# A two-layer hybrid attention trunk: later rotation copies, a value tile between two scores, and four places in the queues

## The chip, the core and the metric

The kernel runs on one core of one Trainium2 chip. The core has a matrix engine (TensorE, "PE" in the profile; its weight loads are listed apart as "PEld"), VectorE ("DVE"), ScalarE ("ACT"), GpSimd ("POOL") and SyncE ("SP"). Each works through its own queue of instructions in the order in which they were put there, and a wait at the head of a queue holds up all behind it. In this kernel SP issues all the DMA transfers; "SPq" is its queue. The metric is the time of one execution of the whole program on the device, in microseconds (us); the median of the runs is given.

## The reference: what is computed

The trunk has two layers over one sequence of 1024 tokens of width 1024, in float32. In each layer a modulated RMSNorm gives `h`, a combined input projection feeds an attention, its output is gated with SiLU, and an output projection with a gate is added to `x`.

```python
for i in range(2):
    shift, scale, gate = modulation(c, ada_w[i], ada_b[i])      # silu(c) @ ada_w + ada_b
    h = rmsnorm(x, norm_g[i]) * (1 + scale) + shift
    y = diff_attention(h, ...) if i == 0 else mla(h, ...)
    x = x + gate * y
return rmsnorm(x, final_norm_g)

def diff_attention(h):                  # 8 heads, two 64-wide query/key pairs, values 128 wide
    q, k, v, z = split(h @ w_in0)
    q, k = rope(q), rope(k)             # x1*cos - x2*sin, x2*cos + x1*sin
    p = softmax(q k^T / 8)
    o = (p[0] - lam * p[1]) @ v
    return (rmsnorm(o) * silu(z)) @ w_out0

def mla(h):                             # 8 heads, 128 + 64 wide
    q_a, c_kv, k_pe, z = split(h @ w_in1)
    q = rmsnorm(q_a) @ w_q_b; k, v = split(rmsnorm(c_kv) @ w_kv_b)
    o = softmax((q_nope k_nope^T + rope(q_pe) rope(k_pe)^T) / sqrt(192)) @ v
    return (o * silu(z)) @ w_out1
```

## The kernel before

**Precision.** Every operand of a product is split into a high part (`fp32r`, made by a cast on ACT) and a low part (the difference, made by a subtraction on POOL or DVE), and a product of two tiles is three matmuls (`mm3`, lines 182 to 184): high by high, high by low, low by high.

**Start (to about 145 us).** `h0`, the transposed modulated input, is made in two halves of 512 tokens. Value tiles (`v0_tile`, line 737: 8 steps of `mm3` each, one tile for each 128 tokens and half of the value columns) are projected, cast by `store_v` (L362, L363) and stored to DRAM. The keys, queries and the gate z of head 0 are projected here. The loop `for tt in range(8)` (line 859) runs the value tiles of the second column half; between them it issues what `pend` holds, the rest of the rotation of head 0, and ahead of tile 6 (`V_LATE`) the score tile `q_tile(0, 0, 0, ...)` of head 0, which takes its banks from a new PSUM pool.

**First attention (to about 692 us).** `attn0` takes the heads in turn. A head has 8 query tiles. `q_tile` (line 837) issues for each of the two query/key pairs four score matmuls (L847), a row maximum on DVE (L400) and an exponential on ACT (L402), then the combination on DVE (L855). Then the tile before it is transposed on PE (L383), copied out by ACT (L385, `pth`) and DVE (L386, `ptl`), and multiplied by the values (`pv`). Between these parts PE gets fill work: `FILL0` says how many steps of `stream0` go where. `stream0` is the projection of the next head's keys, queries and z from `h0`: three strips for each head, two halves of 512 tokens for each strip, 8 steps (one `mm3` each) for each half, 48 steps for each head.

**The rotation.** When a half of keys or queries is complete, `rope` (line 312) copies it out of PSUM on ACT (`rp_raw`, L319 or L321), issues four transfers that exchange the 32-row blocks (`rp_sw`, L323), and multiplies by the cosines (L324). It returns two functions. `rot` multiplies the exchanged rows by the sines (L329) and, where `add` is POOL, adds the two on POOL (L331). `fin` adds them on DVE (L336) where `add` is DVE, and returns the sum `r`. Heads 1 to 7 of the first layer rotate with POOL alone, head 0 with DVE. `stack_k` (line 341) and `stack_q` (line 349) then make the operands of the scores: two casts of 64 rows on ACT (L344, L345; L352, L353), two subtractions on POOL (L346, L347; L354, L355), and for queries four transfers that copy the rows to the other half of the partitions (L357, L358).

**The side list.** `Side` (line 279) is a list from which one entry is taken at each step of `stream0` and once after each query tile; an entry is a function or nothing. `k_done` and `q_done` (lines 752 and 764) put 8 entries on it for each half: three empty, `rot`, three empty, and `g`, which calls `fin` and stacks.

**Order.** The program's order is not kept as it stands on every engine: the instructions are put in order for each engine at compile time by estimated times. `tc.issue_after(ins)` holds the instructions of a block behind `ins` where they are on the same engine; `tc.keep_in_program_order` (`in_turn`) fixes an instruction's place; `behind("S")` and `behind("V")` hold a cast or an addition behind the last softmax or transposed copy that was traced on that engine (`mk`).

**First output projection (about 660 to 790 us).** It is done with seven products of half-size blocks in place of eight (`Seven`). Each product needs operands that are split into high and low (`split_a`, `split_w`: a cast on ACT, L1171, a subtraction on POOL or DVE, L1172). In head 7, where `stream0` has run out, `extra0(i)` runs after query tile `i`: it fetches and splits the first product's operands and, by `PRE0`, issues steps of the first products (`pre0.step()`, one step at tile 4, two at tile 5 and so on).

**Second layer.** `group0` (line 1399) makes the second layer's `h1` for 512 tokens from eight chunks (`h_chunk`, line 459: four transposes on PE, a modulated cast on ACT, L473, the same value on DVE, L477, and a subtraction, L478); those of the first group go through the side list beside the last output products. `lora` (line 1621) projects the latent strips; it loads and splits a strip's weights with `strip1` (L206, then L227 on ACT and L228 on POOL) and needs the first two strips (`w4`, split earlier) before the third. Then `z_pair` (line 1756) makes the gates of three pairs of heads, again with seven products, and `load_wk` (line 1787) loads and splits the value weights, `fh` being the half of the columns: a cast on DVE (L1792), a subtraction on POOL (L1793). Raw weights share two buffers with the tag `wraw`. The second attention (about 976 to 1330 us) and the second output projection follow.

Of the kernel before, what the change touches and what calls it, by code (L numbers as in the profile page):

```python
# [16 lines left out]
ALU = mybir.AluOpType  # L17
# [20 lines left out]
DEF = 7  # L38
ROT = 3
# [5 lines left out]
V_LATE = 6  # L45
# [31 lines left out]
def f32v(ap):  # L77
    return ap.bitcast(F32)
# [3 lines left out]
def trunk(ctx: ExitStack, tc: tile.TileContext, A, out):  # L82
    nc = tc.nc
    SP, PE, V, S, G = nc.sync, nc.tensor, nc.vector, nc.scalar, nc.gpsimd
# [256 lines left out]
    def stack_k(t, r):  # L341

        with behind("S"):
            S.copy(t[0:64, 0, :], r[0:64])  # L344
            S.copy(t[64:128, 1, :], r[64:128])  # L345
        in_turn(G.tensor_sub(t[64:128, 0, :], r[0:64], f32v(t[0:64, 0, :])))  # L346
        in_turn(G.tensor_sub(t[0:64, 1, :], r[64:128], f32v(t[64:128, 1, :])))  # L347

    def stack_q(qa, qb, r):

        with behind("S"):
            S.copy(qa[0:64, 0, :], r[0:64])  # L352
            S.copy(qa[64:128, 1, :], r[64:128])  # L353
        in_turn(G.tensor_sub(qb[0:64, 0, :], r[0:64], f32v(qa[0:64, 0, :])))  # L354
        in_turn(G.tensor_sub(qb[64:128, 1, :], r[64:128], f32v(qa[64:128, 1, :])))  # L355
        for t in (qa, qb):
            SP.dma_start(f32v(t[64:128, 0, :]), f32v(t[0:64, 0, :]))  # L357
            SP.dma_start(f32v(t[0:64, 1, :]), f32v(t[64:128, 1, :]))  # L358
# [393 lines left out]
    def k_done(h):  # L752
        def f(acc, half):
            rot, fin = rope(wp, acc, half, 1.0, *[G if h else V] * 2)

            def g():
                t = a0a.tile([P, 2, HF], F32R, name="ks", tag="ks", bufs=4)
                stack_k(t, fin())
                KS.setdefault(h, [None, None])[half] = t

            side.add(*[None] * ROT, rot, *[None] * (DEF - 1 - ROT), g)
        return f

    def q_done(h):
        def f(acc, half):
            rot, fin = rope(wp, acc, half, SC0, *[G if h else V] * 2)

            def g():
                qa = a0a.tile([P, 2, HF], F32R, name="qa", tag="qs", bufs=4)
                qb = a0a.tile([P, 2, HF], F32R, name="qb", tag="qs", bufs=4)  # L770
                stack_q(qa, qb, fin())
                QS.setdefault(h, [None, None])[half] = qa, qb

            side.add(*[None] * ROT, rot, *[None] * (DEF - 1 - ROT), g)
        return f

    def silu_gate(tp, acc):

        th = tp.tile([P, HF], F32, name="zth", tag="rp", bufs=6)
        gz = wst.tile([P, HF], F32, name="gz", tag="gz", bufs=3)  # L780
        S.activation(th, acc, AF.Tanh, scale=0.5)
        V.scalar_tensor_tensor(out=gz, in0=th, scalar=1.0, in1=acc, op0=ALU.add, op1=ALU.mult)
        return gz

    def z_done(h):
# [73 lines left out]
    for tt in range(8):  # L859
        if tt == V_LATE:  # L860
            psum("ps2", sc=2, tr=1, pv=1)
            zz0 = sm.tile([P, 4], F32, name="zz")
            first += [zz0, q_tile(0, 0, 0, zz0, a0a)]
        for _ in range(MODS[tt]):
            next(mods_g)
        for t in pend[2 + 2 * tt : 4 + 2 * tt] if tt else ():
            t()
        v0_tile(tt, 1, wv1)
    assert next(mods_g, 0) == 0
    stm.close()  # L870

# [394 lines left out]
    def extra0(i):  # L1266
        nonlocal xp, pw
        if i < 4:
            gate_step0()
        if i == 1:  # L1270
            sv0.fetch_w(0, 0)
        if i < Z_LAST:
            return
        sv = sv0

        def fa(n, *hs):
            for h in hs:
                sv.fetch_a(n, h)

        def fw(n, *hs):  # L1280
            for h in hs:
                sv.fetch_w(n, h)

        def both(n, h):
            sv.split_a(n, h, G)
            sv.split_w(n, h)

        if i == Z_LAST:
            stream0.step(99)
            side.flush()  # L1290
            stW.close()
            stH.close()
            xp = pool(stX, "xp", side="right")
            pw = pool(stO, "pw0", side="right")
            k0["o"] = pw.tile([P, HF], F32, name="o7")
            k0["sq"] = wst.tile([P, HF], F32, name="sq7", tag="gz", bufs=3)
            for n in ("11", "21", "12"):
                k0[n] = pw.tile([P, HF], F32, name="k" + n)
            sv.kept[0][3], sv.kept[1][3] = k0["11"], k0["12"]
            fa(0, 0, 1)  # L1300
            fw(0, 1)
            sv.split_w(0, 0)
        if i == 3:
            sv.split_a(0, 0, G)
            fw(0, 2)
            fa(0, 2)
            fw(0, 3)
            tc.keep_in_program_order(SP.dma_start(k0["11"], oF[0][3, 0]))
        for n, h in ((), (), (), (), ((0, 1), (0, 2)), ((0, 3),), ((1, 0), (1, 1)), ((1, 2),), (), (), ())[i]:
            both(n, h)  # L1310
        while rests:
            rests.pop(0)()
        if i == 4:
            for h in range(2):
                fw(1, h)
                fa(1, h)
        if i == 5:
            fw(1, 2)
            fa(1, 2)
            fw(1, 3)  # L1320
        if i == 6:
            tc.keep_in_program_order(SP.dma_start(k0["21"], oF[0][3, 1]))
            k0["pair"] = [pw.tile([P, HF], F32, name="ob", tag="ob", bufs=4) for _ in range(4)]
            for t, (hh, half) in zip(k0["pair"], ((2, 0), (6, 0), (2, 1), (6, 1))):
                tc.keep_in_program_order(SP.dma_start(t, oF[0][hh, half]))
        if i == 8:
            sv.split_w(1, 3)
            a11, a12, a21, a22 = k0["pair"]
            for n, t in ((2, a11), (3, a22), (4, a12), (5, a21)):
                sv.kept[n][2] = t  # L1330
            k0["sum"] = combine(*k0["pair"])
        if i > 7:
            next(k0["sum"], None)
        for _ in range(PRE0[i]):
            pre0.step()
# [44 lines left out]
    def strip1(i, wpool=None):  # L1380
        return load_strip([A["w_s1"][i, f] for f in range(2)], [4, 4], wpool)
# [17 lines left out]
    def group0(gi):  # L1399
        fulls = [[x_] for x_ in xf[4 * gi : 4 * gi + 4]]  # L1400
        V.tensor_add(ssa[gi], ssa[gi], ssb[gi])
        norm_x(ssa[gi], fulls, (2, 3) if gi else (1, 3))

        def chunk(k):
            if gi == 1:
                h1[k][1] = xt2k("h1h"), xt2k("h1l")
                h1f[k] = ut(f"h1f{k}", dt=F32)
            else:
                h1[k][0] = [h1p.tile([P, HF], F32R, name="h1_" + x_, tag="h1", bufs=16) for x_ in "hl"]
            lm["V"] = h_chunk(1, fulls, k, h1[k][gi], p3x, V, f32=h1f[k] if gi else None)  # L1410

        if gi == 0:
            side.add(*[None] * G_WAIT)
        side.add(*[lambda k=k: chunk(k) for k in ((0, 4, 1, 5, 2, 6, 3, 7) if gi else range(KT))])
# [206 lines left out]
    def lora(idx, dst, gvec, width, ws=None, first=None):  # L1621
# [45 lines left out]
            norms.append(lambda: norms.append(rest))  # L1667

        for i, si in enumerate(idx):
            w = strip1(si) if i or ws is None else ws  # L1670
            for half in range(2):
                if (i, half) == (0, 0) and first:
                    first(lambda acc: put(0, 0, acc))
                else:
                    half_and_norm(w, half, lambda acc: put(i, half, acc))
                if i == n - 1:
                    norms.append(lambda half=half: norm(half))
# [109 lines left out]
    def load_wk(fh):  # L1787
        for k in range(2):
            raw = wst.tile([P, HF], F32, name="wvr", tag="wraw", bufs=2)
            SP.dma_start(raw, A["w_v1"][k, fh])  # L1790
            h_, l_ = [pv1.tile([P, HF], F32R, name="wv" + x_, tag="wv1", bufs=4) if fh else ut("wv" + x_, True) for x_ in "hl"]
            V.tensor_copy(h_, raw)  # L1792
            G.tensor_sub(l_, raw, f32v(h_))  # L1793
            wk[k][fh] = (h_, l_)

    def v1_tile(tt, fh, sp, *buf):
# [17 lines left out]
    def late_z(i):  # L1814
        if i == 0:
            load_ck(CK, 3, [(k, half) for half in range(2) for k in range(2)])
            for name, nk in (("w_qr", 3), ("w_kn", 2), ("w_qn", 3)):
                raw = p4.tile([P, HF], F32, name="zraw", tag="zraw", bufs=6)
                SP.dma_start(raw[:, : nk * P], A[name][0])
                kraw.append((raw, nk))  # L1820
        if i == 2:
            load_wk(0)
            load_ck(CQ, 0, [(i, half) for half in range(2) for i in range(3)])
            load_wk(1)

    z_pair(1)
    z_pair(2)
    z_pair(3, late_z)
    ws1 = [split_strip([raw]) for raw in kraw]
# [536 lines left out]
```

## Time and profile before

| | |
|---|---|
| time, median of 3 runs | 1434.04 us (1433.14 to 1435.34) |
| the profiled execution's own time | 1429.06 us |
| its span, first to last instruction | 1426.9 us |
| mean granted clock of TensorE | 0.992 |
| ACT, share of the span | 737.9 us, 52% |
| POOL, share of the span | 753.9 us, 53% |
| DMA, share of 16 engines' span | 51.0% |

Busy times come from the hardware profiler. Matmuls are pipelined, and their ends are modelled, so a busy PE can hide short gaps: a 128x512 matmul is listed with some 0.39 us, while the next one starts 0.22 us after it. In a row of the timeline the columns are the start and the length in us, the engine, the line, the operation, the tile written and the tiles read, shapes and count; in brackets how long the engine had stood idle and who ended that. In a row of the waits they are who waited (engine, tile, line) and for whom, then us in total, the number of waits and the longest. A row of the windows has the stretch, its length, the busy us of the five engines with their counts of instructions, the granted clock (1.00 is full), the share of the DMA engines and GB/s.

### The profile page before, as it was taken

The page shows a single profiled execution, that of the slowest core. Times are in us where ns is not written, and L with a number is a line of the kernel's source. Part 1 is how long each engine was busy: PE and PEld are TensorE (multiplying, and loading weights), DVE is VectorE, ACT ScalarE, POOL GpSimd, SP SyncE. Part 2 cuts the span into 40 slices and gives each one's busy share as a digit, 9 for nine tenths or more (in the row PEclk, how much of TensorE's full clock was granted, in tenths as well). Part 3 has the DMA queues.
Part 4 walks back from the last instruction along what each step waited for, and adds up shares of the span by engine and source line. Part 5 has one row for each costly group of instructions (what it writes and reads, how often), then busy time and mean ns, then how long its engine had stood idle before and what let it go on. Part 6 is the DMA issues. An engine that isn't in the chain of part 4 may idle for free.

```text
span 1426.9 us, 20750 instructions
## 1 busy us (share of the span) xinstructions
PE 1380.7 (97%) x7350; PEld 1150.1 (81%) x7350; DVE 937.0 (66%) x1337; ACT 737.9 (52%) x1331; POOL 753.9 (53%) x592
## 2 busy tenths in 40 slices
PE   8999999999999999999998999999999999999997
PEld 6767787888878788787786888887888888888886
DVE  7665668776766666667596886545666655555685
ACT  5523455655555556566555544335454454545554
POOL 5415263758685858576695232543131165653783
PEclk8999999999999999999999999999999999999999
DMA  9776634343434344425574126398544355566463
GB/s 341 250 237 191 203 91 116 103 143 90 155 116 131 122 135 132 139 70 173 174 252 155 45 75 229 109 305 251 159 124 121 102 162 189 181 212 205 141 246 119
DMA packets 149066, 231.54 MB, mean 162 GB/s; under 512 B 20577, under 2 KB 57569, under 8 KB 148962
## 3 DMA queue, kind: packets, MB, share of 16 engines
q1 hardware_dynamic: 148962, 230.21, 51.0%
q8 instruction: 58, 0.95, 0.3%
q14 instruction: 46, 0.38, 0.1%
HBM read 144.74 MB, written 61.81 MB: 145 GB/s over the span
## 4 chain that ended last, share of the span: by engine, by line
PE 70%; DVE 5%; POOL 5%; ACT 3%; DMA 3%; issue 2%; SPq 2%; POOLq 0%; ACTq 0%; DVEq 0%
PE s L1986 10%; PE acc L182 8%; PE acc L184 8%; PE acc L183 8%; PE tr L383 7%; PE s L847 6%; PE pv L182 3%; PE pv L184 3%; PE pv L183 3%; PE zacc L184 1%; PE zacc L183 1%; PE zacc L182 1%; PE oy L184 1%; PE oy L182 1%; PE oy L183 1%
## 5 line engine op out<-in xcount | busy, mean ns | idle before, releaser
L385 ACT CAST pth<-tr 128x512 fp32r<-128x512 f32 x256 | 150.1, 586 | 283.8 <-PE tr L383 280.6
L400 DVE TENSOR_REDUCE nm<-s 128x1 f32<-128x1024 f32 x192 | 233.9, 1219 | 77.4 <-PE s L847 68.1
L386 DVE TENSOR_TENSOR ptl<-tr,pth 128x512 fp32r<-128x512 f32 x256 | 176.1, 688 | 148.5 <-ACT pth L385 147.9
L228 POOL TENSOR_TENSOR wl<-wraw,wh 128x512 fp32r<-128x512 f32 (+2 forms) x79 | 102.1, 1295 | 185.0 <-ACT wh L227 180.8
L383 PE MATMUL tr<-ident,e 128*128 128x128 f32 x1024 | 155.8, 274 | 10.0 <-DVE ptl L386 9.7
L383 PEld LDWEIGHTS tr<-ident,e 128*128 128x128 f32 x1024 | 120.4, 140 | 54.3 <-DVE ptl L386 31.5
L402 ACT ACTIVATE e<-s,nm 128x1024 f32<-128x1024 f32 x128 | 143.6, 1121 | 26.5 <-DVE nm L400 26.2
L182 PE MATMUL acc<-h0h,wh 128*128 128x512 f32 x360 | 150.6, 418 | 0.1
L182 PE MATMUL pv<-pth,vt 128*128 128x256 f32 x512 | 147.5, 288 | 0.0
L183 PE MATMUL pv<-ptl,vt 128*128 128x256 f32 x512 | 145.5, 284 | 0.0
L184 PE MATMUL pv<-pth,vt 128*128 128x256 f32 x512 | 144.6, 282 | 0.0
L184 PE MATMUL acc<-h0h,wl 128*128 128x512 f32 x360 | 143.2, 398 | 0.4 <-POOL wl L228 0.4
L183 PE MATMUL acc<-h0l,wh 128*128 128x512 f32 x360 | 142.1, 395 | 0.0
L183 PEld LDWEIGHTS pv<-ptl,vt 128*128 128x128 f32 x512 | 97.6, 191 | 2.9
L182 PEld LDWEIGHTS pv<-pth,vt 128*128 128x128 f32 x512 | 97.4, 190 | 3.1 <-ACT pth L385 0.2
L184 PEld LDWEIGHTS pv<-pth,vt 128*128 128x128 f32 x512 | 97.6, 191 | 0.0
L329 POOL TENSOR_TENSOR rp_sw<-rp_sw,sinT 128x512 f32<-128x512 f32 x42 | 57.3, 1365 | 73.8 <-DMA rp_sw<-rp_raw 72.8
L324 POOL TENSOR_TENSOR rp_r<-rp_raw,cosT 128x512 f32<-128x512 f32 x38 | 49.8, 1312 | 86.4 <-ACT rp_raw L321 38.7
L1172 POOL TENSOR_TENSOR wol<-wol,woh 128x512 fp32r<-128x512 f32 x56 | 82.8, 1500 | 21.5 <-ACT woh L1171 18.8
L847 PE MATMUL s<-ks,qa 128*128 128x512 f32 x256 | 83.5, 407 | 5.9 <-DVE e L855 4.1
L855 DVE SCALAR_TENSOR_TENSOR e<-s,z,e 128x1024 f32<-128x1024 f32 x64 | 82.2, 1284 | 2.2
L847 PE MATMUL s<-ks,qb 128*128 128x512 f32 x256 | 80.7, 396 | 0.3 <-DMA qb<-qb 0.3
(411 smaller groups left out, 3484.3 us busy)
## 6 DMA issues: line engine op xcount, KB each, us to landing
ada<-in_ada_ss SPq DMA_DIRECT2D x32, 512.0 KB, 5.6
wraw<-in_w_s SPq DMA_DIRECT2D x64, 256.0 KB, 2.9
vS<-v_hl SPq DMA_DIRECT2D x32, 512.0 KB, 6.0
vt<-vS SPq DMA_DIRECT2D x32, 512.0 KB, 4.7
wol<-tS SPq DMA_DIRECT2D x56, 256.0 KB, 5.1
tS<-ob SPq DMA_DIRECT2D x48, 256.0 KB, 2.0
rp_sw<-rp_raw SPq DMA_DIRECT2D x168, 64.0 KB, 2.0
bc_s<-bc_d SPq DMA_DIRECT2D x34, 256.0 KB, 3.9
```

Of the source, the lines that this page charges most:

```text
L182: PE.matmul(psum, ah, bh, start=first, stop=False, skip_group_check=skip)
L183: PE.matmul(psum, ah, bl, start=False, stop=False, skip_group_check=skip)
L184: mm3.last = PE.matmul(psum, al, bh, start=False, stop=last, skip_group_check=skip).ins
L228: sub = (V if pair_of else G).tensor_sub(l_[:, :n], raw[:, :n], f32v(h_[:, :n]))
L383: transpose_p.last = PE.transpose(tr[:, j, :], p[:, kt * P : (kt + 1) * P], ident).ins
L385: mk["S"] = S.copy(pth[kh][:, :, dst], tr).ins
L386: mk["V"] = V.tensor_sub(ptl[kh][:, :, dst], tr, f32v(pth[kh][:, :, dst])).ins
L400: mk["V"] = V.reduce_max(nm, s_ps, axis=AX.X, negate=True).ins
L402: mk["S"] = S.activation(e, s_ps, AF.Exp, bias=nm, scale=1.0, accum_out=zs).ins
L847: PE.matmul(s_ps[:, kc * HF : (kc + 1) * HF], src[:, c, ql], KS[h][kc][:, c, :], start=fst, stop=not fst)
L1172: sub = eng.tensor_sub(lo, raw, f32v(hi))
L1986: PE.matmul(s_ps[:, kc * HF : (kc + 1) * HF], lhs, rhs(kc), start=i == 0, stop=i == 4)
```

## The change

For heads 1 to 7, `k_done` and `q_done` put two more entries on the side list ahead of `g`: one that calls `fin`, and an empty one, which the queries of heads 5 to 7 do without. In the start stage a value tile is put between the two scores of the first query tile, and `pend`'s functions are held behind the last gate product. In head 7 three splits change places. In `lora` the casts of all strips that it loads itself are held behind the ACT cast of the first group's last chunk. The value weights `fh = 1` are loaded one stage earlier, and their subtraction is on DVE.

```diff
@@ k_done
-                stack_k(t, fin())
+                stack_k(t, r.pop() if r else fin())
-            side.add(*[None] * ROT, rot, *[None] * (DEF - 1 - ROT), g)
+            r = []
+            sum_ = [lambda: r.append(fin()), None] if h else []
+            side.add(*[None] * ROT, rot, *[None] * (DEF - 1 - ROT), *sum_, g)
@@ q_done
-                stack_q(qa, qb, fin())
+                stack_q(qa, qb, r.pop() if r else fin())
-            side.add(*[None] * ROT, rot, *[None] * (DEF - 1 - ROT), g)
+            r = []
+            sum_ = [lambda: r.append(fin()), None][: 1 + (h < 5)] if h else []
+            side.add(*[None] * ROT, rot, *[None] * (DEF - 1 - ROT), *sum_, g)
@@ silu_gate
-        V.scalar_tensor_tensor(out=gz, in0=th, scalar=1.0, in1=acc, op0=ALU.add, op1=ALU.mult)
+        silu_gate.last = V.scalar_tensor_tensor(out=gz, in0=th, scalar=1.0, in1=acc, op0=ALU.add, op1=ALU.mult).ins
@@ for tt in range(8)
-            first += [zz0, q_tile(0, 0, 0, zz0, a0a)]
+            first += [zz0, q_tile(0, 0, 0, zz0, a0a, lambda c: None if c else v0_tile(V_LATE, 1, wv1))]
...
-            t()
-        v0_tile(tt, 1, wv1)
+            with tc.issue_after(silu_gate.last):
+                t()
+        if tt != V_LATE:
+            v0_tile(tt, 1, wv1)
@@ extra0
         if i == 3:
-            sv.split_a(0, 0, G)
...
-        for n, h in ((), (), (), (), ((0, 1), (0, 2)), ((0, 3),), ((1, 0), (1, 1)), ((1, 2),), (), (), ())[i]:
+        if i == 4:
+            sv.split_a(0, 0, G)
+            both(0, 1)
+            sv.split_a(0, 2, G)
+        if i == 5:
+            sv.split_w(0, 2)
+        for n, h in ((), (), (), (), (), ((0, 3),), ((1, 0), (1, 1)), ((1, 2),), (), (), ())[i]:
             both(n, h)
@@ group0, chunk
+            if gi == 0:
+                lm["h"] = h_chunk.act
@@ lora
-            w = strip1(si) if i or ws is None else ws
+            w = ws
+            if i or ws is None:
+                raws = fetch_strip([A["w_s1"][si, f] for f in range(2)], [4, 4])
+                with tc.issue_after(lm["h"]):
+                    w = split_strip(raws)
@@ load_wk
-            G.tensor_sub(l_, raw, f32v(h_))
+            (V if fh else G).tensor_sub(l_, raw, f32v(h_))
@@ late_z
             load_ck(CQ, 0, [(i, half) for half in range(2) for i in range(3)])
-            load_wk(1)
...
     z_pair(1)
+    load_wk(1)
     z_pair(2)
```

`both(n, h)` is `split_a(n, h, G)` and `split_w(n, h)`.

## The prediction

> **What bounds the kernel now.** I read the page first, then the list of waits, then windows by stage, and last the timeline around the stalls that the change touches.
>
> ```profile
> span 1426.9 us, 20750 instructions
> ...
> PE 1380.7 (97%) x7350; PEld 1150.1 (81%) x7350; DVE 937.0 (66%) x1337; ACT 737.9 (52%) x1331; POOL 753.9 (53%) x592
> ```
>
> TensorE (PE) is the bound from end to end: 1380.7 of 1426.9 us. No matmul is added or removed, so the change can only win from the 46 us in which PE stands, and from matmuls run at a lowered clock. The waits of PE and the two of ScalarE (ACT) that matter most (who waited for whom: us in total, times, longest):
>
> ```profile
> PE tr L383 <- DVE ptl L386: 9.7, 11, 2.2
> PE trh L468 <- DVE h L477: 4.5, 1, 4.5
> PE s L847 <- DVE e L855: 4.1, 7, 1.0
> PE ssq L924 <- ACT rp_raw L321: 2.5, 1, 2.5
> PE vps L182 <- DVE gz L782: 1.3, 1, 1.3
> PE s L847 <- DVE v_hl L363: 1.3, 1, 1.3
> PE acc L182 <- ACT rp_raw L321: 1.2, 1, 1.2
> ...
> PE vps L182 <- DVE v_hl L363: 0.7, 1, 0.7
> ...
> ACT qa L352 <- POOL rp_r L331: 23.3, 11, 4.8
> ACT ks L344 <- POOL rp_r L331: 8.2, 5, 3.4
> ```
>
> The pattern: ACT's queue is served in order, and the casts that stack a rotated half (qa, ks) stand at its head while GpSimd (POOL) still makes the rotation's sum, 31.5 us in all. Behind them stand the exponentials and the copies of transposed tiles (pth), on which DVE's ptl and e depend, and on these PE. The windows (length, then PE, PEld, DVE, ACT and POOL busy, granted clock, DMA share, GB/s) say where PE pays:
>
> ```profile
> 206.00:224.00 18.00, 14.24 (x80) 11.35 (x79) 12.83 (x17) 7.93 (x14) 9.14 (x8) 1.00 0.49 121
> ...
> 412.00:420.00 8.00, 5.50 (x26) 4.39 (x25) 4.62 (x9) 4.90 (x8) 7.77 (x7) 0.87 0.47 149
> ...
> 478.00:512.00 34.00, 30.74 (x159) 23.82 (x158) 23.68 (x33) 20.05 (x37) 26.37 (x22) 1.00 0.47 140
> ...
> 562.00:582.00 20.00, 17.57 (x94) 14.10 (x93) 12.85 (x18) 10.74 (x19) 14.31 (x13) 1.00 0.38 108
> ...
> 655.00:712.00 57.00, 51.45 (x303) 42.33 (x302) 37.62 (x59) 35.70 (x64) 36.47 (x31) 1.00 0.55 178
> ...
> 776.00:780.00 4.00, 2.96 (x10) 2.52 (x11) 3.79 (x6) 2.20 (x5) 0.20 (x1) 0.57 0.57 193
> ...
> 945.00:960.00 15.00, 15.00 (x68) 12.43 (x67) 8.34 (x13) 6.21 (x11) 3.60 (x3) 1.00 1.07 352
> ```
>
> Idle PE in the first four (length less PE busy): 3.76, 2.50, 3.26 and 2.43, together 11.95 us, all within the first attention. At 412 to 420 the clock was 0.87 as well, 8 x 0.13 = 1.0 us of matmul time lost.
>
> **1. The copies two steps later (heads 1 to 7).** For these heads the sum is already issued by `rot`, so the new list entry only returns the tile: no instruction is added, the stacking casts, their two POOL subtractions and, for queries, four SP transfers move back by two ticks of the side list (one for queries from head 5 on). A tick comes with each of 48 stream steps and 8 tiles of a head; the first qb score of head 6 stands at 569.62 and of head 7 at 640.31 (rows below), 70.7 us for 56 ticks, 1.26 us each. Each half's list grows from 8 entries to 10, against 9.3 ticks per half, so the list backs up by a step or two within a head and `rot` moves a little too.
>
> ```profile
> 211.90 0.62 ACT L352 CAST qa<-rp_r 64x512 fp32r<-64x512 f32 x1 [4.80 <-POOL rp_r L331]
> ...
> 412.40 0.62 ACT L352 CAST qa<-rp_r 64x512 fp32r<-64x512 f32 x1 [2.42 <-POOL rp_r L331]
> ...
> 415.40 0.59 ACT L321 ACTIVATE rp_raw<-acc 128x512 f32<-128x512 f32 x1
> ```
>
> In the first, ACT stood 4.80 us with an exponential queued behind it. In the second, rp_raw, which frees the accumulator that PE's ssq waits for, ran only at 415.40. 2.5 us of delay remove most such waits (31.5 us over 16 waits is 2.0 each). Of 11.95 + 1.0 I leave 0.25 (a DMA wait, below) and 1.5 for the longer waits cut but not ended: gain 11.2.
>
> [...]
>
> The price. With the shift, the list runs the query casts of half 0 in the same step as the end of half 1, behind half 1's rp_raw on ACT, its cosine product on POOL, and its four rp_sw transfers on SP. The shifted rows are needed by the next head's first score:
>
> ```profile
> 633.75 0.60 ACT L321 ACTIVATE rp_raw<-acc 128x512 f32<-128x512 f32 x1 [0.16 <-PE acc L184]
> ...
> 636.80 0.46 SPq L358 DMA_DIRECT2D qb<-qb  x1
> ...
> 637.99 2.44 SPq L323 DMA_DIRECT2D rp_sw<-rp_raw  x4
> ...
> 640.31 0.62 PE L847 MATMUL s<-ks,qb 128*128 128x512 f32 x2
> ...
> 566.33 0.46 SPq L358 DMA_DIRECT2D qb<-qb  x1
> ...
> 569.62 0.62 PE L847 MATMUL s<-ks,qb 128*128 128x512 f32 x2
> ...
> 495.59 0.46 SPq L358 DMA_DIRECT2D qb<-qb  x1
> ...
> 498.40 0.47 PE L847 MATMUL s<-ks,qb 128*128 128x512 f32 x1 [0.25 <-DMA qb<-qb]
> ...
> qb<-qb SPq DMA_DIRECT2D x32, 128.0 KB, 2.3
> ```
>
> Head 7: rp_raw ends at 634.35, four rp_sw take 2.44, three shifts 0.55 each before the last: it is issued at 638.45 and lands 2.3 later at 640.75, 0.4 after its use at 640.31. Heads 5 and 6: the last issue moves from 495.59 and 566.33 by the same 1.7 or so, to 497.3 and 568.0, lands at 499.6 and 570.3: 1.45 after 498.15 (where PE already waited) and 0.7 after 569.62. Together 2.5 us. The shifts of heads 1 to 4 have had more time before their scores, and I cost them at nothing. In return rp_sw leaves some 3 us earlier (for head 7 at 634.4 in place of 637.99), and the second half's sum is ready sooner. ACT also gets rp_raw and two casts in one piece, 0.60 + 2 x 0.62 us, ahead of an exponential: I allow 1.4 us over all heads. **Net gain 11.2 - 2.5 - 1.4 = 7.3**; bounds 13 (no price) and a loss of 1 (half the gain, 7 for late queries).
>
> **2. The value tile between the two first scores.** The 1.27 us of the wait "s <- v_hl" is a PSUM bank of an earlier value tile, freed late. The tile put between issues up to 24 matmuls, 0.22 us each where PE runs without a break (the window at 945 to 960: 15.00 us, 68 of them), 5.3 us of cover: gain 1.3, bounds 0 and 1.4.
>
> **3. The wait behind the gate product.** DVE runs the rotary add before gz, whose bank PE awaits:
>
> ```profile
> 124.45 0.69 DVE L336 TENSOR_TENSOR rp_r<-rp_r,rp_sw 128x512 f32<-128x512 f32 x1 [2.42 <-POOL rp_sw L329]
> 125.06 0.68 DVE L782 SCALAR_TENSOR_TENSOR gz<-zth,acc 128x512 f32<-128x512 f32 x1
> ...
> 128.66 0.68 DVE L782 SCALAR_TENSOR_TENSOR gz<-zth,acc 128x512 f32<-128x512 f32 x1
> ...
> 132.07 1.28 POOL L354 TENSOR_TENSOR qb<-rp_r,qa 64x512 fp32r<-64x512 f32 x1
> ```
>
> With the places exchanged gz starts up to 0.61 earlier, and more, since it need not wait for the add's POOL product (2.42 us of DVE's time); what its own tanh allows I take as 1.0 of the 1.3 us that PE waited: gain 1.0. Both adds of head 0's queries now wait for the second gz, to 129.3 if it stays where it is; behind them wait the qa casts on ACT, then POOL, which reaches their subtraction only at 132.07, so it is hidden. Without that cover it would cost about 1. Bounds -1 and +1.3.
>
> **4. The third strip's cast.** In the same view of the timeline:
>
> ```profile
> 770.49 0.60 ACT L227 CAST wh<-wraw 128x512 fp32r<-128x512 f32 x1
> 774.24 0.62 ACT L227 CAST wh<-wraw 128x512 fp32r<-128x512 f32 x1 [3.14 <-DMA wraw<-in_w_s]
> ...
> 775.38 1.43 ACT L473 ACTIVATE h_h<-trh,modb,moda 128x512 fp32r<-128x512 f32 x2
> ...
> 777.04 1.12 PE L468 MATMUL trh<-ident,x 128*128 128x128 f32 x4 [4.50 <-DVE h L477]
> ```
>
> ACT waits 3.14 us for a strip that is multiplied much later (four half strips of 24 matmuls at 0.22 us, 21 us, come first), while h_h waits behind it and PE for DVE's h. With the cast behind the chunks, 3.14 plus the cast's 0.52 go: PE waits some 0.8 instead of 4.50. At 776 to 780 the clock was 0.57, 1.7 us lost; the chunks' own chain sets half of that pace, so I add 0.6. **Gain 4.3**, bounds 2 (next strip's load, which needs the raw buffer, becomes late) and 5.4. SP's load of that next strip now waits some 10 us for the buffer, with the x1 stores queued behind it, which nobody awaits here.
>
> **5. The V weights of the second MLA layer.** Their two loads (512 KB) leave the stretch at 945 to 960, whose DMA share is 1.07, and two subtractions go from POOL to DVE at about 0.69 each:
>
> ```profile
> L1733 DVE TENSOR_TENSOR zraw<-zs,zraw 128x512 f32<-128x512 f32 x3 | 2.1, 693 | 1.2 <-POOL wl L228 1.1
> ```
>
> PE was fully busy in this window. Just after it stand the waits "acc <- rp_raw" (1.2) and "vps <- v_hl" (0.7), behind an SP queue full of stores; both gone is the upper bound, 1.9. If DVE's two added subtractions came late for a product of the pair it would be -1 (an estimate: 2 x 0.69 less what DVE has free). I take 0.6.
>
> **6. Head 7's splits.** The first A split moves one tile later, next to its use, and one W split moves a tile on: as many ACT casts and POOL subtractions as before. This stage idles 5.55 us of 57 for lack of fill work. The third matmul of the first product now waits for a cast and a POOL subtraction that stand right before it; PE's order can put other work there. I take 0, bounds -1.5 and +1.
>
> **Sum.** 7.3 + 1.3 + 1.0 + 4.3 + 0.6 + 0 = 14.5 us. The profiled execution took 1429.06 us with a span of 1426.9 and would take 1414.6; the timed median is 1434.04, 5.0 above it, and I carry the difference over: **1419.5 us**.
>
> **Rivals.**
> - *The waits move along with the copies.* POOL, not the list, sets the time: it is 53% busy in all and 7.77 of 8 us at 412 to 420. Then the sum is late again behind the shifted subtractions, part 1 gives 0, and the rest 7.2: 1426.8. Against it: from its place two steps on, a cast has 2.5 us more than a mean wait needs.
> - *Everything comes off.* Part 1 at 13, part 4 at 5.4, 2 and 3 at 1.3 and 5 at 1.9: 23 us, 1411.
> - *Late queries decide: slower.* In heads 5 to 7 the casts now stand behind a rp_raw that itself waits for PE's last matmul of the half. If the reordering puts that a tile (70.7 / 8 = 8.8 us) further back, qb comes up to 8 us after each of three first scores: 24 us against 14.5, 1443.5. It decides from 4.8 us per head on. For it: head 5 waits already (0.25), 6 and 7 have 1 us of margin. Against it: rp_raw waited only 0.16 for PE.
> - *The order stays what it was.* The entries return a tile and the planner may issue as before: 1434. The moved casts are fixed behind the last pth or exponential traced, so this hardly holds for part 1.
>
> **How the numbers follow.** Forecast 0.58 (its own range 1413 to 1426), waits moving along 0.18, everything 0.10, slower 0.09, no effect 0.05. The range 1410 to 1430 takes in the first three and leaves out some 0.18. A measurement tells about 0.2% from no change, 2.9 us: faster is below 1431.2, which holds for the first three cases, less 0.02: 0.84; same 0.06; slower 0.10.
>
> **What would show it.** ACT's qa and ks casts should wait for rp_r under 10 us in all, not 31.5, and PE should stand little at 206 to 224 and 412 to 420; "PE trh <- DVE h" should fall under 1.5; the waits "vps <- gz" and "s <- v_hl" should go. A new wait "s <- DMA qb" of 2 to 3 us in all is the price. If that wait exceeds 10 us, or ACT still waits 20 us for rp_r, the prediction is wrong in part 1.

## The result, and the profile after

The changed kernel took 1424.16 us (median of 6 runs, 1421.18 to 1424.97) beside 1432.77 for the kernel before (6 runs). The ratio of all runs is 0.9933, 95% interval 0.992 to 0.9946: 9.6 us less, between 7.7 and 11.5 (the means are 1423.5 and 1433.1; the two medians differ by 8.6). The forecast was 14.5 less, 1419.5, in a range of 1410 to 1430. The profiled execution took 1421.18 us, 7.9 less than the profiled one of before (1429.06); both are among the fastest of their kernel.

The page of the changed kernel first, then its list of PE's waits (who waited for whom: us in total, times, longest):

```profile
span 1419.2 us, 20732 instructions
...
PE 1382.2 (97%) x7350; PEld 1152.0 (81%) x7350; DVE 939.5 (66%) x1339; ACT 736.9 (52%) x1331; POOL 752.1 (53%) x590
```

```profile
PE s L851 <- DMA qa<-qa: 4.5, 4, 2.3
PE tr L383 <- DVE ptl L386: 2.8, 5, 0.9
PE vps L182 <- DVE v_hl L363: 2.3, 1, 2.3
PE oy L184 <- POOL oal L1178: 1.7, 2, 1.2
PE s L851 <- DVE e L859: 1.7, 3, 1.0
PE oy L183 <- POOL wol L1178: 1.7, 3, 1.1
PE trh L468 <- DVE h L477: 1.6, 2, 0.9
...
PE vps L182 <- DVE gz L786: 1.5, 1, 1.5
...
PE s L851 <- DMA qb<-qb: 0.8, 2, 0.5
...
PE trh L468 <- ACT x L455: 0.3, 1, 0.3
...
PE trh L468 <- DVE x L457: 0.2, 1, 0.2
```

The three waits that came of ScalarE's stalls (tr for ptl, first scores for e, ssq for rp_raw) summed to 9.7 + 4.1 + 2.5 = 16.3 us. They are 2.8 + 1.7 + 0 = 4.5 now. In their place stands the wait of the first scores for the shifted query rows: 4.5 + 0.8 = 5.3, against 0.3. ScalarE's own stalls, from its list of waits:

```profile
ACT qa L352 <- DVE rp_r L336: 3.2, 1, 3.2
...
ACT qa L352 <- POOL rp_r L331: 2.4, 2, 1.6
ACT ks L344 <- POOL rp_r L331: 0.4, 1, 0.4
```

From 31.5 to 2.8 us for POOL's sum; the 3.2 for DVE's sum is new and belongs to part 3. The windows of the changed kernel (length, then PE, PEld, DVE, ACT and POOL busy, granted clock, DMA share, GB/s):

```profile
206.00:224.00 18.00, 18.00 (x99) 15.24 (x98) 14.45 (x22) 11.31 (x20) 9.25 (x8) 1.00 0.46 119
404.00:412.00 8.00, 8.00 (x44) 6.46 (x43) 5.96 (x9) 5.55 (x11) 7.76 (x7) 1.00 0.16 54
470.00:504.00 34.00, 33.12 (x182) 27.50 (x181) 22.06 (x33) 20.26 (x36) 25.13 (x22) 1.00 0.49 140
553.00:573.00 20.00, 17.74 (x90) 14.56 (x89) 11.36 (x18) 10.29 (x18) 10.22 (x9) 0.91 0.36 93
```

The first three have nearly lost their idle time (9.5 us before, 0.9 now); the fourth (head 6's scores to come) is as idle as before (2.26 us, 2.43 before) and has a lowered clock besides (0.91, 1.00 before).

Line by line, from PE's two lists of waits (after less before): the three waits above -11.8, the query rows +5.0, the wait "s <- v_hl" -1.3, "vps <- gz" +0.2, "trh <- h" -2.9 with +0.5 for x in the same transposes, "acc <- rp_raw" -1.2 and "vps <- v_hl" +1.6, "oy <- oal" +0.9 and "oy <- wol" +1.1. The sum is -7.9, and the spans differ by 7.7. That they agree so closely is in part luck: the other lines of the two lists give another -1.4 (half of it at 12 us, where the change does nothing), and PE's busy time rose by 1.5, from 1380.7 to 1382.2.

### The profile page after: what moved, and what is told of

Its sections match the earlier page's. It is cut to its first block, busy times and chain, and to the rows that moved or that the text cites. A ratio compares the mean times of both kernels' runs of the same rounds, so it can differ in the third digit from the quotient of the medians.

```text
span 1419.2 us, 20732 instructions
## 1 busy us (share of the span) xinstructions
PE 1382.2 (97%) x7350; PEld 1152.0 (81%) x7350; DVE 939.5 (66%) x1339; ACT 736.9 (52%) x1331; POOL 752.1 (53%) x590
```

## The experiments

Each kernel was timed in several rounds against the kernel before, 4 to 12 executions each. The table has the ratio with its interval, PE's wait for the query rows (DMA qa + qb), the sum of the three waits of ScalarE's stalls, and how often the clock went to half speed for 3.4 us in the profile (last section; from windows of 2 us between 140 and 1040).

| kernel | ratio | 95% interval | query rows, us | three waits, us | half speed |
|---|---|---|---|---|---|
| before | 1 | | 0.3 | 16.3 | 2 |
| changed | 0.9933 | 0.9920 to 0.9946 | 5.3 | 4.5 | 2 |
| e1, part 1 alone | 0.9928 | 0.9912 to 0.9945 | 6.4 | 6.0 | 2 |
| e2, without part 1 | 1.0002 | 0.9989 to 1.0015 | 0.2 | 16.1 | 4 |
| e3, without part 5 | 0.9926 | 0.9908 to 0.9944 | 6.6 | 4.4 | 1 |
| e4, without part 6 | 0.9927 | 0.9906 to 0.9948 | 7.3 | 6.6 | 1 |
| e5, first halves early | 0.9919 | 0.9899 to 0.9939 | 4.3 | 6.4 | 1 |
| e6, two steps for all | 0.9944 | 0.9925 to 0.9963 | 7.2 | 6.3 | 3 |
| e7, keys alone late | 0.9953 | 0.9937 to 0.9968 | 1.6 | 10.7 | 2 |
| e8, parts 1, 2, 4 | 0.9913 | 0.9892 to 0.9934 | 7.0 | 6.0 | 2 |
| e9, lists merged | 0.9960 | 0.9947 to 0.9974 | 2.1 | 7.0 | 3 |
| e10, parts 1, 2, 4, merged | 0.9893 | 0.9876 to 0.9909 | 1.8 | 6.5 | 1 |
| e11, parts 2 and 4 alone | 0.9976 | 0.9962 to 0.9989 | 0.8 | 16.3 | 3 |
| e12, merged from head 5 on | 0.9880 | 0.9859 to 0.9900 | 2.2 | 7.0 | 1 |

**Which part carries the time (e1, e2, e11).** e1 is the kernel before with the edits of k_done and q_done; e2 is the changed kernel without them; e11 is the kernel before with these two edits:

```diff
-            first += [zz0, q_tile(0, 0, 0, zz0, a0a)]
+            first += [zz0, q_tile(0, 0, 0, zz0, a0a, lambda c: None if c else v0_tile(V_LATE, 1, wv1))]
...
-            w = strip1(si) if i or ws is None else ws
+            w = ws
+            if i or ws is None:
+                raws = fetch_strip([A["w_s1"][si, f] for f in range(2)], [4, 4])
+                with tc.issue_after(lm["h"]):
+                    w = split_strip(raws)
```

> The kernel before with part 1 alone (copies of heads 1 to 7 behind the sum). My theory: part 1 carries most of the gain, 7 to 8 us net: ratio to before 0.9945 to 0.9955, about 1425.5; ScalarE's waits for rp_r fall from 31.5 to under 5 us and the new waits of the first scores for the shifted query rows (DMA qa, qb) come to 5 or 6 us; the wait trh <- h of 4.5 us stays. Rival, the waits only move along: ratio 0.998 to 1.0, and the rp_r waits or POOL waits near 30 us. Rival, late queries decide: ratio above 1.0.

> The changed kernel with part 1 undone, parts 2 to 6 kept. My theory: 1.5 to 2.5 us are left of the gain (third strip's cast 3, value tile 1.3, against 1 each lost by the V weights and the head 7 splits): ratio to before 0.998 to 0.999, about 1430.5; the rp_r waits are back at about 30 us and the DMA qa and qb waits gone. By the sum of the prediction the other parts are worth 7.2: ratio 0.995. Rival, the waits only move along: as fast as the changed kernel, 0.9933.

> The kernel before with parts 2 and 4 alone. By the stages of the traces the third strip's cast brings 1.5 to 2.6 us and the value tile about 0.5: ratio to before 0.9975 to 0.9985; by the prediction 4.3 + 1.3: 0.996; if parts 2 to 6 cancel because part 4 itself brings nothing: 1.000.

Part 1 alone brings 10.3 us (7.9 to 12.6), as much as the whole change. Without it nothing is left (1.0002), fewer than the 1.5 to 2.5 us that I had expected from the trace, and the "7.2" of the forecast is refuted. Parts 2 and 4 alone bring 3.4 us (1.6 to 5.4). So parts 3, 5 and 6 together cost the difference of e2 and e11, 0.0026 or 3.7 us (about 1 to 6.4, from the two intervals; each was timed against the kernel before in its own rounds). e2's list of waits of ScalarE shows that the stalls come back whole:

```profile
ACT qa L352 <- POOL rp_r L331: 22.8, 11, 4.8
ACT ks L344 <- POOL rp_r L331: 8.2, 5, 3.4
```

The rival "the waits only move along" falls with e1 and e2 together.

**The small parts one by one (e3, e4).** e3 puts load_wk(1) and POOL's subtraction back; e4 puts head 7's split_a and split_w back:

```diff
-            (V if fh else G).tensor_sub(l_, raw, f32v(h_))
+            G.tensor_sub(l_, raw, f32v(h_))
...
+            load_wk(1)
...
-    load_wk(1)
     z_pair(2)
```

```diff
+            sv.split_a(0, 0, G)
             fw(0, 2)
...
-        if i == 4:
-            sv.split_a(0, 0, G)
-            both(0, 1)
-            sv.split_a(0, 2, G)
-        if i == 5:
-            sv.split_w(0, 2)
```

> The changed kernel with the V weights' loads and subtractions as before (part 5 undone). The trace of the changed kernel says part 5 costs 1 us (vps <- v_hl rose from 0.75 to 2.35): then 1 us faster than changed, ratio to before 0.9925, and that wait is back at about 0.75 with acc <- rp_raw back at about 1.2. By the prediction's step (gain 0.6): 0.6 slower than changed, 0.9937.

> The changed kernel with head 7's splits in their places of before (part 6 undone). If part 6 makes the waits of head 7's output products (oy <- oal 1.7, oy <- wol 1.1 us) then those fall by about 1 us and the ratio to before is 0.9925; if part 6 is neutral as predicted, 0.993 and those waits stay; if it hides something, 0.994 or more.

The ratios (0.9926 and 0.9927 beside 0.9933) are too close to decide by themselves; the waits do. Without part 5, PE's list has the two small waits of before again in place of the one of 2.3:

```profile
PE acc L182 <- ACT rp_raw L321: 1.2, 1, 1.2
...
PE vps L182 <- DVE v_hl L363: 0.8, 1, 0.8
```

Without part 6, the output products wait less (1.7 and 1.7 in the changed kernel). The kernel before first, then e4:

```profile
PE oy L184 <- POOL oal L1172: 0.8, 1, 0.8
...
PE oy L183 <- POOL wol L1172: 0.6, 2, 0.3
```

```profile
PE oy L184 <- POOL oal L1178: 0.7, 1, 0.7
...
PE oy L183 <- POOL wol L1178: 0.6, 2, 0.3
```

That is 0.3 us for part 5 (2.3 less 1.2 + 0.8) and 2.1 for part 6 (3.4 less 1.3). The kernel without parts 3, 5 and 6:

> The changed kernel without the wait behind the gate product, the V weights' move and the head 7 splits (parts 1, 2 and 4 alone). My theory from the stages of the traces: part 5 costs 1.4 and part 6 2, the gate's wait nothing: 3 us faster than changed, ratio to before 0.991, about 1420. By the prediction (1.0 + 0.6 + 0 for these three): 1.6 slower than changed, 0.9945.

e8 has 0.9913: in the direction of my second thoughts and not of the forecast, though its interval meets that of the changed kernel.

**Why the first scores wait (e5, e6, e7).** Three edits of the list's length, in this order:

```diff
-            sum_ = [lambda: r.append(fin()), None][: 1 + (h < 5)] if h else []
+            sum_ = [lambda: r.append(fin()), None] if h and (half or h < 5) else []
```

```diff
-            sum_ = [lambda: r.append(fin()), None][: 1 + (h < 5)] if h else []
+            sum_ = [lambda: r.append(fin()), None] if h else []
```

```diff
-                stack_q(qa, qb, r.pop() if r else fin())
+                stack_q(qa, qb, fin())
...
-            side.add(*[None] * ROT, rot, *[None] * (DEF - 1 - ROT), *sum_, g)
+            side.add(*[None] * ROT, rot, *[None] * (DEF - 1 - ROT), g)
```

> The changed kernel, but in heads 5 to 7 the first half of the queries is copied where it was before (no step later); its second half gets two steps. My theory: the first scores of heads 5 to 7 no longer wait for the shifted query rows (0.6, 2.3 and 1.2 us in the changed kernel's trace; DMA qa and qb waits fall from 5.3 to about 1.2, head 4's), and ScalarE's waits for rp_r come back by about 2.5 (561 us and 631 us in the trace of before), which cost PE about 0.7: net 2.5 to 3.5 faster than changed, ratio to before 0.991. Rival (the first score of a head waits for something else as well): within 1 us of changed.

> The changed kernel with two steps for the queries of heads 5 to 7 as well. My theory, late queries are what part 1 costs: one step is 1.26 us, so the first scores of heads 5, 6 and 7 wait about 1.3 longer each, 2.5 to 4 slower in all, ratio to before 0.995 to 0.996, DMA qa and qb waits 8 to 9 us. Rival (the issue order of SP alone sets the landing, not the step): no change, 0.993.

> The changed kernel with the queries' copies as before, the keys' two steps later. Of the 31.5 us that ScalarE waited for rp_r, 8.2 were for keys and 23.3 for queries. My theory: the queries carry most of the gain: ratio to before 0.998 to 0.9995 (without part 1 it was 1.0002, keys alone bring 1 to 2.5 us, at the stall of 1.6 us at 479), qa waits near 23, ks waits under 1. Rival (any relief of POOL and ScalarE helps alike): half of part 1's gain, 0.9965.

None of the three came out as I had expected. In e5 the first half had no step of its own (and the second half two, one more than in the change). Heads 5 to 7 still waited 2.7 us for the query rows where I had expected nothing; with head 4's 1.6, which the edit leaves alone, that is 4.3. With a step more (e6) the first scores waited 7.2 and not 8 to 9, and the ratio 0.9944 can't be told from 0.9933: inconclusive. In e7 the queries had their old entries, and yet a first score waited 1.6 us for qa, and ScalarE's wait for the queries' sum fell from 23.3 to 17.0; the kernel (0.9953) kept 0.0049 of the 0.0069 that lie between e2 and the changed kernel, about what the rival said (its 0.9965 is within the interval) or more. So the queries' copies move even where nobody moves them. What moves them should be the list itself: it is served in order, one entry per tick. A key's half now takes 10 entries where 9.3 ticks come, so 1.3 ticks are left over when the queries' entries are added. The timeline of SP in the changed kernel shows what a late copy meets (start, duration):

```profile
551.81 0.32 SPq L408 DMA_DIRECT2D bc_d<-rq_y  x1
553.04 0.33 SPq L206 DMA_DIRECT2D wraw<-in_w_s  x1
553.47 1.15 SPq L323 DMA_DIRECT2D rp_sw<-rp_raw  x2
554.70 0.53 SPq L410 DMA_DIRECT2D bc_s<-bc_d  x1
555.29 1.14 SPq L323 DMA_DIRECT2D rp_sw<-rp_raw  x2
556.53 0.54 SPq L357 DMA_DIRECT2D qa<-qa  x1
557.12 0.59 SPq L358 DMA_DIRECT2D qa<-qa  x1
```

Four transfers of the other half's rp_sw stand ahead of the first qa. In PE's timeline, its score:

```profile
560.86 1.01 PE L851 MATMUL s<-ks,qa 128*128 128x512 f32 x2 [2.26 <-DMA qa<-qa]
```

**The test of the leftover ticks (e9, e10, e12).** The list gets a second way to add: entry by entry into the ticks that are already taken. In e9 all queries of heads 1 to 7 use it, with the change's own steps. e10 has parts 1, 2 and 4 alone, the same merge, and for heads 5 to 7 no step for the first half and two for the second. e12 is e10 with the merge from head 5 on. The edits of e9, of e10 to its list and of e12 to the line that adds:

```diff
+        def merge(self, *entries):
+            for i, e in enumerate(entries):
+                if i < len(self.q):
+                    self.q[i] = lambda a=self.q[i], e=e: [f() for f in (a, e) if f]
+                else:
+                    self.q.append(e)
...
-            side.add(*[None] * ROT, rot, *[None] * (DEF - 1 - ROT), *sum_, g)
+            (side.q and h and side.merge or side.add)(*[None] * ROT, rot, *[None] * (DEF - 1 - ROT), *sum_, g)
```

```diff
+            sum_ = [lambda: r.append(fin()), None][: 0 if h > 4 and not half else 2] if h else []
```

```diff
+            (side.merge if h > 4 else side.add)(*[None] * ROT, rot, *[None] * (DEF - 1 - ROT), *sum_, g)
```

> The changed kernel, but the queries' entries of the side list no longer queue behind what is left of the keys' longer entries: they are merged with it, tick by tick. The list takes 10 entries per half of a key against 9.3 ticks, so a key half leaves 0.7 of a tick and two of them 1.3 ticks, 1.7 us, by which the first half of the next head's queries is late beyond its own step. My theory now (this backlog, not the queries' own step, makes the first scores wait): the DMA qa and qb waits of heads 4 to 7, 5 to 6 us in the traces with part 1, fall to 2.5 us or less, the rp_r waits stay under 6 us, and the ratio to before is 0.991. Rival (SP's order, the four rp_sw ahead, sets the landing): the waits stay at 5 us and the ratio at 0.993.

> Parts 1, 2 and 4 alone with the merged list, and the first half of the queries of heads 5 to 7 with no step of its own. My theory: its copies then come at the same tick as in the kernel before, so the first scores of heads 5 to 7 do not wait (DMA qa and qb 1.5 us or less, head 4's), and with the V weights and the splits in their old places 4 us less than the changed kernel: ratio 0.990, about 1418. Rival (what is saved at the first scores comes back as waits of ScalarE for rp_r, 2 us each): no faster than parts 1, 2 and 4, 0.9915 to 0.993.

> Parts 1, 2 and 4 with the list merged for heads 5 to 7 alone (head 4 and before as in the changed kernel), first half of the queries of heads 5 to 7 with no step of its own. My theory: in the two kernels with the merged list PE stood 2.2 to 2.5 us at 360 us for a weight product of POOL (acc <- wl), where head 4's merged entries crowd POOL; without the merge there that wait goes, and head 3's stage takes 69.7 instead of 73.2 us: ratio to before 0.987 to 0.988, about 1414. Rival (that wait is unrelated to the merge, or comes back as a longer DMA qa wait at head 4): 0.989 as with the merge everywhere.

The waits answer as the leftover ticks would have it: in e9 the first scores' wait for the query rows fell to 2.1 us, 1.8 of it at head 4. The time did not follow: 0.996, slower than the changed kernel. ScalarE waited 9.8 us for rp_r where I had expected under 6, and PE's list of e9 names a new wait, POOL being late with a weight product:

```profile
PE acc L184 <- POOL wl L228: 2.5, 1, 2.5
```

It begins at 364 us in e9 and at 360 in e10, where it is 2.2. e12 leaves heads 1 to 4 out of the merge, and nothing is left of it: the one wait of this name in e12 is elsewhere, in the start, where e1 and e8 have it too.

```profile
105.26 0.50 PE L184 MATMUL acc<-h0h,wl 128*128 128x512 f32 x1 [0.46 <-POOL wl L228]
```

So that wait came with the merge in the early heads. Which head's entries cause it is not shown: I had said head 4's, but in e10 the subtractions that POOL makes just ahead of it (356.37 to 359.0 us) are those of head 3's queries. For heads 5 to 7 the SP queue of e12 has the order of the kernel before again, qa ahead of rp_sw:

```profile
553.72 0.50 SPq L364 DMA_DIRECT2D qa<-qa  x1
554.52 0.33 SPq L206 DMA_DIRECT2D wraw<-in_w_s  x1
554.95 0.50 SPq L365 DMA_DIRECT2D qa<-qa  x1
...
558.32 1.81 SPq L330 DMA_DIRECT2D rp_sw<-rp_raw  x3
```

e12 is the fastest of all, 0.988 (0.9859 to 0.99), 1416.09 us, 17 us less than the kernel before; its interval lies below that of the changed kernel. Both ratios are as I had expected, and e10's rival (0.9915 at best) is refuted. But e10 and e12 can't be told apart by their ratios, though e12 lacks the wait of 2.2: its list has a new one of 2.5 for stored values ("pv <- DMA vt"). What the merge is worth in time is less sure than what it does to the waits: e8 has the same parts without it, and e10's interval meets e8's, while e12 is 0.0033 lower (about 0.0004 to 0.006). e9 is 3.9 us slower than the changed kernel by its ratio. The new wait of 2.5 would cover part of that; the rest stays open.

## Why the prediction was right, and where it was not

The direction, the main cause and the range held: the copies two steps later take most of the time, since ScalarE no longer stands ahead of its exponentials (2.8 us of waits for POOL's sum in place of 31.5). The time came out 4.7 us above the forecast, nearer than its parts, whose errors offset each other in part. By the ratios of the groups, parts 3, 5 and 6 came out 5.3 worse than forecast (a gain of 1.6 that was a loss of 3.7), parts 2 and 4 2.2 worse, and part 1 3.0 better.

**Part 1** was forecast at 7.3. Alone it measured 10.3 (7.9 to 12.6), so 7.3 is just outside. In the traces of before and changed the gross gain is 11.8 of PE's waits against 11.2 forecast, in which 1.0 was for the clock. The price of the late query rows was mis-sized: 2.5 forecast, 5.0 measured (6.1 in e1). I had written that the list "backs up by a step or two" and gave it no price; I counted the query's own step alone. The runs showed the backlog to be what delays the rows. The shifts of heads 1 to 4, which I "cost at nothing", include head 4's, which kept its scores waiting 1.2 us in the changed kernel and 1.8 in e9. The 1.4 that I allowed for casts in one piece shows in no wait.

Twice the price and yet a larger gain: the waits do not add up to the time. They come to 11.8 - 5.0 = 6.8 in the changed kernel and to 10.3 - 6.1 = 4.2 in e1, whose profiled execution was 6.8 us faster than that of before, while the timed runs say 10.3. The profiled execution of before was about 4 us faster than the median of its kernel, so what the missing 3.5 us are is in no trace. The clock can be a part of it: in e1's rounds the mean granted clock was 0.9948 for e1 and 0.9914 for before. If TensorE were the bound at every moment, that would be 4.9 us (an estimate, and the most that it can be). How much it is stays open.

**Part 2** was right: "s <- v_hl" is gone, 1.3 us. **Part 4** was too large: 4.3 forecast, 4.5 - 1.6 - 0.5 = 2.4 in the waits. I gave PE one wait of 0.8 behind the chunks' chain; there are two, of 0.74 and 0.90, and the later transposes wait for x besides. Of the slow stretch at 776 us, 1.7 us, I had counted 0.6; it lies there in both profiles without part 4 (before, and e1 at 768, twice as long) and in none of the twelve with it. On the other side the wait "oy <- x" just ahead of the chunks is 1.6 in nine of those twelve, e11 among them, and 0.5 without part 4; why is not known. Parts 2 and 4 were 5.6 together in the forecast and 3.4 in e11.

**Part 3** was the step that failed: forecast +1.0, measured -0.2. The timeline of the changed kernel, DVE and ACT:

```profile
123.41 0.69 DVE L324 TENSOR_TENSOR rp_r<-rp_raw,cosT 128x512 f32<-128x512 f32 x1 [2.62 <-POOL ks L347]
124.02 1.44 DVE L827 TENSOR_TENSOR lam<-lam 128x64 f32<-128x64 f32 x2
125.38 0.33 DVE L828 TENSOR_REDUCE lp<-lam 128x1 f32<-128x64 f32 x2
125.64 0.67 DVE L786 SCALAR_TENSOR_TENSOR gz<-zth,acc 128x512 f32<-128x512 f32 x1
```

```profile
122.53 1.28 ACT L785 ACT_TABLE_LOAD   x1
124.13 0.60 ACT L785 ACTIVATE zth<-acc 128x512 f32<-128x512 f32 x1 [0.33 <-DVE rp_r L324]
```

In the kernel before, the last cosine product of head 0's queries had its place well ahead:

```profile
112.91 0.69 DVE L324 TENSOR_TENSOR rp_r<-rp_raw,cosT 128x512 f32<-128x512 f32 x1
```

The rotary add did leave its place ahead of gz. Into that place on DVE came this cosine product, which waited 2.62 us for POOL's `ks` subtraction, and behind it the lambda products, to 125.71. Why it moved is argued, not shown: its tile comes from a ring of six buffers (the tag `rp`), which the held-back adds keep longer, and tanh's output is of the same ring (it waited 0.33 us for that product). Tanh ended at 124.73 (124.13 and 0.60), so about 0.9 of the 1.0 that I took was there to be had; the queue gave it to others. I had priced what leaves the place and not what moves in. The qa casts wait 3.2 us for the add in return, which shows in no wait of PE. Without part 3 (e1, e8) "vps <- gz" is 1.3 again, with it 1.5.

**Part 5** was forecast +0.6. "acc <- rp_raw" went as I said, but "vps <- v_hl" rose from 0.75 to 2.35 where I had it vanish: a loss of 0.3 to 0.4, whose cause stays open. **Part 6** was taken at 0 with a bound of -1.5, and it cost 2.0 in the waits. The third matmul of the first product, which I had named, waited only 0.51. The larger part is the W split that moved a tile on: POOL ended its subtraction at 676.55, and PE stood 1.10 for it.

```profile
666.63 0.50 PE L184 MATMUL oy<-woh,oal 128*128 128x512 f32 x1 [0.51 <-POOL oal L1178]
...
676.60 0.50 PE L183 MATMUL oy<-wol,oah 128*128 128x512 f32 x1 [1.10 <-POOL wol L1178]
```

The other 0.4 is at 700.94, a wait of before that grew from 0.83 to 1.24. PE's order put nothing in between: the bound was too narrow, and the middle was the wrong end of it.

Of what would show it, ScalarE's waits under 10 us (2.8), "trh <- h" near 1.5 (1.6), PE's little idle time in the first two windows and the lost "s <- v_hl" came; "vps <- gz" stayed, and the new wait was 5.3 rather than 2 to 3.

## What to carry to other kernels

A list that gives out one entry per tick has a length that must fit its ticks: entries added for one tile delay the next tile's, and the delay is to be priced where the last consumer stands, with the transfers that it then meets on the issuing queue (here four rp_sw, 2.29 us on SP). Price a reordering by what moves into the freed place, not by what leaves it (in part 3, a product that itself waited 2.62 us). Edits that look like small change (three of six here) can together take back a quarter of the gain, so time them as a group against the main edit alone.

## What the runs showed of the hardware that I had not expected

Between 140 and 1040 us of the profiles, lost clock comes in one size: 3.4 us at 0.50, which is 1.7 us, one to four times in each (in e1 and e11 twice in one piece). Behind the same idle time of PE, 2.24 us, it comes in one run and not in another. In the kernel before, the gap and the windows around it (columns as above):

```profile
218.07 0.66 PE L383 MATMUL tr<-ident,e 128*128 128x128 f32 x4 [2.24 <-DVE ptl L386]
```

```profile
216.00:218.00 2.00, 0.00 (x0) 0.00 (x0) 1.97 (x4) 1.07 (x3) 0.79 (x1) 1.00 0.43 98
218.00:220.00 2.00, 1.93 (x11) 1.67 (x12) 2.00 (x3) 0.59 (x1) 1.99 (x2) 1.00 0.16 37
220.00:222.00 2.00, 1.74 (x8) 1.08 (x6) 2.00 (x3) 0.00 (x0) 0.00 (x0) 1.00 0.62 228
```

And of e11, the same place with the same gap:

```profile
215.79 0.66 PE L383 MATMUL tr<-ident,e 128*128 128x128 f32 x4 [2.24 <-DVE ptl L386]
```

```profile
216.00:218.00 2.00, 2.00 (x10) 1.67 (x9) 2.00 (x2) 0.59 (x1) 1.70 (x2) 0.78 0.35 60
218.00:220.00 2.00, 2.00 (x6) 1.54 (x6) 2.00 (x4) 0.04 (x1) 0.00 (x0) 0.50 0.74 238
220.00:222.00 2.00, 2.00 (x12) 1.65 (x11) 1.66 (x2) 1.67 (x4) 0.00 (x0) 0.87 0.69 235
```

In the kernel before the clock stays at 1.00 behind this gap; in e11 the three windows (0.78, 0.50 and 0.87) lose 1.7 us together. The idle time of PE alone does not tell, then, whether the clock goes down; what decides it is not shown.

So the 1.0 us of clock that I put into part 1 comes to nothing between the two profiles: the stretch at 418 us of the kernel before (1.7 us when it is taken whole) went, and another came at 561 in the changed kernel, behind the wait of 2.26 us for qa. Between 140 and 1040 us both profiles have two such stretches, and the difference of the profiles owes nothing to these. The start is another matter: both lose 5.1 us in one piece from 8 us on, and the changed kernel 1.7 more from 103.6 us on. How much of this is paid in time is not shown. Of the six executions of the changed kernel the fastest, 1421.18 us, has the lowest mean clock, 0.991, and the one with the highest, 0.997, took 1423.93. So the mean clock does not by itself tell the time.
